# Second mixer of a two-layer encoder: a head's eight 64-by-64 products in two visits to TensorE instead of four

## The chip, the cores and the metric

One Trainium2 chip, one of its cores. The metric is the device time in microseconds (us) of one execution of the whole program. A core has TensorE (PE in the profile; its weight loads have a row of their own, PEld), VectorE (DVE), ScalarE (ACT), GpSimd (POOL) and SyncE (SP), which here issues the loads of weights. Each engine works through its own instructions in the order in which the program holds them, and semaphores tie the engines together.

## The reference

A trunk of two layers over 256 tokens of width 2048, all in float32. A layer is a token mixer and a gated MLP with a short convolution, each behind an RMSNorm and with a residual. The first mixer is a bidirectional mLSTM, the second, which is touched here, a bidirectional HGRN2 with 16 heads of 128 keys and 128 values:

```python
def hgrn_mixer(hn, w_in, lb, head_g, w_out):
    b, s, _ = hn.shape
    p = hn @ w_in
    q, i, g, f_f, f_b = jnp.split(p, [B_F, B_F + B_V, B_F + 2 * B_V, 2 * B_F + 2 * B_V], axis=-1)
    log_lb, log_1mlb = jnp.log(lb), jnp.log1p(-lb)

    def gate(f):
        f = f.astype(jnp.float32)
        log_f = jnp.logaddexp(log_lb, log_1mlb + jax.nn.log_sigmoid(f))
        k = (1.0 - lb) * jax.nn.sigmoid(-f)
        return (k.reshape(b, s, B_HEADS, B_DK), log_f.reshape(b, s, B_HEADS, B_DK))
    ...
    y = hgrn_direction(q, k_f, lf_f, v) + fl(hgrn_direction(fl(q), fl(k_b), fl(lf_b), fl(v)))
    y = y.reshape(b, s, B_V).astype(hn.dtype)
    y = head_rmsnorm(y, head_g, B_HEADS) * jax.nn.silu(g)
    return y @ w_out
```

In each direction a head's output at token t is the sum over the tokens s before it (and t itself) of v[s], weighted by the sum over keys of q[t] k[s] times the product of all forget gates between s and t.

## The kernel before

All the large products (projections, MLPs) take float32 weights from memory in pieces of 128 by 1024. ACT rounds a piece to `wh` (L146), the DVE makes the rest `wl` (L147), and TensorE multiplies both with activations that are split the same way. There are four buffers each for `wh` and `wl` (WB). The projections run in chunks: "fm" chunks (features by tokens, L197 and L198, four contraction tiles in a piece) and "tm" chunks (tokens by features, L187 to L189, two in a piece). In the second mixer each of four groups of four heads has six "fm" chunks (q and two gates a head), one "tm" chunk for the values ahead of the fourth of them, and one "tm" chunk for the output gate at the end. These chunks are the dense matmuls of this text.

Beside the dense stream runs side work, written as generators. A `yield` hands over how much later the generator goes on; the stream's clock (`side.tick`) moves by a fixed amount with each contraction tile. A scheduler that comes with the language then orders the instructions of each engine by its own estimate of times, so the order on an engine isn't quite that of the code.

The side work of a head (function `head` in `hgrn`) computes the 128-by-128 attention blocks AT without ever dividing by a product of gates. It goes up a tree of block sizes h = 1, 2, 4, ... 64 (LEVELS). At each level the DVE multiplies the q and k of half of the blocks by the gates of the neighbouring half (the scalings, L648 and L649, in place in QK), POOL multiplies gates pairwise to those of twice the block size (L654), and the DVE gathers the needed halves to fresh buffers `km` and `qm` (L606). TensorE then forms from them a product of four 64-by-64 matmuls into `pd` (L614). A product of q with ks, the sum of both directions' keys, gives the diagonal; ACT copies it to AD (L632), and the six levels below 64 are merged in by predicated copies under a mask (L640, DVE). The seventh level and AD go to AT on ACT (L643, L644). With the products for q and ks that makes eight products a head, 128 in all.

They are sent in four visits: the diagonal with level 1, then levels 2 and 4, 8 and 16, 32 and 64, and between visits the DVE works on the next two levels. A visit's turn comes `2 * SPREAD` ticks after the one before (`2 * STEP` for the last two heads). The gathers have four buffers each (MIX). After the fourth visit come two 128-by-128 products for the tokens of the other half (L658, L659, the state products), then, once the values are there, the y products (L671), a head norm, the output gate (L686), a transpose `pz` (L692) and the split into `yb` (L204, L205), the input of the output projection. Heads don't wait for each other: head 1 is pushed when its last gate is there, while head 0 is on its way, and so on in pairs.

Of the kernel before, what the change touches and what calls it, by code (L numbers as in the profile page):

```python
# [8 lines left out]
F32 = mybir.dt.float32  # L9
F32R = mybir.dt.float32r  # L10
I32 = mybir.dt.int32
AF = mybir.ActivationFunctionType
ALU = mybir.AluOpType
PSUM = bass.MemoryType.PSUM

P = 128
T = 256
# [6 lines left out]
BH = 16  # L24
# [15 lines left out]
STEP = 1.9  # L40
SPREAD = 2.4
LOOK = 3
RAW = 3
WB = 4
MIX = 4
FIRST = (0, 1, 2, 4, 7, 10, 13, 16)

HALF = 64
LEVELS = (1, 2, 4, 8, 16, 32, HALF)
C_ID, C_MF, C_MB, C_LV = 0, 128, 384, 640  # L50
# [3 lines left out]
def trunk_kernel(ctx, tc, xT, pp_d, cst_d, w_first, w_aq, w_ak, w_av, w_ao, w_aout,  # L54
                 w_bq, w_bv, w_bg, w_bout, w_up, w_down, out, mscr, stop=9):
    nc = tc.nc
    act, dve, pool, pe = nc.scalar, nc.vector, nc.gpsimd, nc.tensor
# [8 lines left out]
    cst = keep.tile([P, NCST], F32, name="cst")  # L66
# [11 lines left out]
    def aux(name):  # L78
        return psa.tile([P, 512], F32, tag="aux", name=name)
# [132 lines left out]
    def fm_scaled(ps, R, dst, scale=None):  # L212
        fm_sum(ps, dst)
        if scale is None:
            dve.tensor_tensor(dst, dst, R, ALU.mult)
        else:
            dve.scalar_tensor_tensor(dst, dst, scale, R, ALU.mult, ALU.mult)
# [75 lines left out]
    def head_scale(ss, width):  # L293
        rs = ev.tile([P, 2], F32, tag="rs", bufs=6, name="rs")
        dve.tensor_scalar(rs, ss, 1.0 / width, EPS, ALU.mult, ALU.add)
        pool.tensor_tensor(rs, rs, hmx, ALU.pow)
        return rs
# [238 lines left out]
    def hgrn(norm, nxt):  # L536
# [24 lines left out]
        def blocks(z, h, a, b):  # L561
            v = z[:, 0:2 * (T + h)].rearrange("k (p x) -> k p x", p=2)[:, :, a:b]
            return v.rearrange("k p (m j) -> k m p j", j=2 * h)[:, :, :, 0:h]

        def gview(g, n, start, h):
            v = g[:, start:start + 2 * (n - 1)].rearrange("k (p x) -> k p x", p=2)[:, :, 0::2]
            return v.rearrange("k p m -> k m p").unsqueeze(3).broadcast_to([P, n // 2, 2, h])

        def take(hd, what, ps):
            mp = box["mp"]  # L570
            st = heads[hd]
            if what == 0:
                st["q"] = mp.tile([P, T], F32, tag="q", bufs=2, name="q")
                fm_scaled(ps, norm.R, st["q"], box["oml"][:, hd:hd + 1])
                st["QK"] = mp.tile([P, 1152], F32, tag="QK", bufs=2, name="QK")
                st["G"] = mp.tile([P, 768], F32, tag="G0", bufs=2, name="G")
                return
            dr = what - 1
            lb, oml = box["lb"], box["oml"]
            QZ, KZ, G = st["QK"][:, 0:512], st["QK"][:, 512:1024], st["G"]  # L580
            z = mp.tile([P, T], F32, tag="z", bufs=2, name="z")
            fm_scaled(ps, norm.R, z)
            g = G[:, dr * T:(dr + 1) * T]
            kz = KZ[:, dr * T:(dr + 1) * T]
            act.activation(g, z, AF.Sigmoid)
            act.activation(kz, z, AF.Sigmoid, scale=-1.0)
            dve.tensor_scalar(g, g, oml[:, hd:hd + 1], lb[:, hd:hd + 1], ALU.mult, ALU.add)
            pool.tensor_tensor(QZ[:, (1 - dr) * T:(2 - dr) * T], st["q"], g, ALU.mult)
            if dr == 0:
                pool.tensor_copy(G[:, 512:768], g)  # L590
            else:
                st["ks"] = mp.tile([P, T], F32, tag="ks", bufs=2, name="ks")
                pool.tensor_tensor(st["ks"], KZ[:, 0:T], KZ[:, T:2 * T], ALU.add)
                side.push(head(hd))

        def head(hd):
            mp = box["mp"]
            st = heads[hd]
            QZ, KZ = st["QK"][:, 0:640], st["QK"][:, 512:1152]
            q, ks, G = st["q"], st["ks"], st["G"]  # L600
            AT = mp.tile([P, 4, P], F32, tag="AT", bufs=2, name="AT")
            AD = mp.tile([P, 2, HALF], F32, tag="AD", bufs=2, name="AD")

            def gather(z, h, tag):
                m = mp.tile([P, T], F32, tag=tag, bufs=MIX, name=tag)
                dve.tensor_copy(m.rearrange("k (m p j) -> k m p j", p=2, j=h), blocks(z, h, 0, T))  # L606
                return m

            def product(pd, k, q, flip=0):

                for b in range(4):
                    o, c = b % 2 * HALF, b // 2 * HALF
                    e = b ^ flip
                    pe.matmul(pd[o:o + HALF, c:c + HALF], k[:, b * HALF:(b + 1) * HALF], q[:, e * HALF:(e + 1) * HALF],  # L614
                              start=True, stop=True)

            def both(ps):
                return ps.rearrange("p (a b) -> p a b", a=2)

            step = 2 * (SPREAD if hd < BH - 2 else STEP)  # L620
            ms = [(gather(KZ, 1, "km"), gather(QZ, 1, "qm"))]
            n = T
            for v in range(4):
                pd = aux("pd")
                if v == 0:
                    product(pd[:, 0:P], ks, q)
                for i, (km, qm) in enumerate(ms):
                    h = LEVELS[max(0, 2 * v - 1) + i]
                    w = i if v else 1
                    product(pd[:, w * P:(w + 1) * P], km, qm, h == HALF)  # L630
                if v == 0:
                    act.copy(AD, both(pd[:, 0:P]))  # L632
                for i in range(len(ms)):
                    li = max(0, 2 * v - 1) + i
                    h = LEVELS[li]
                    w = i if v else 1
                    src = both(pd[:, w * P:(w + 1) * P])
                    if h < HALF:
                        mask = cst[:, C_LV + li * HALF:C_LV + (li + 1) * HALF].bitcast(I32)
                        dve.copy_predicated(AD, mask.unsqueeze(1).broadcast_to([P, 2, HALF]), src)  # L640
                    else:
                        for o in (0, HALF):
                            act.copy(AT[o:o + HALF, 0::3, HALF - o:P - o], src[o:o + HALF])  # L643
                            act.copy(AT[o:o + HALF, 0::3, o:o + HALF], AD[o:o + HALF])  # L644
                ms = []
                for h in LEVELS[2 * v:2 * v + 2] if v < 3 else LEVELS[6:]:
                    qa, ka = blocks(QZ, h, 0, T), blocks(KZ, h, 0, T)
                    dve.tensor_tensor(ka, ka, gview(G, n, 1, h), ALU.mult)  # L648
                    dve.tensor_tensor(qa, qa, gview(G, n, n + 1, h), ALU.mult)  # L649
                    if h < HALF:  # L650
                        ms.append((gather(KZ, 2 * h, "km"), gather(QZ, 2 * h, "qm")))
                        n //= 2
                        G2 = mp.tile([P, 3 * n], F32, tag=f"G{h}", bufs=2, name="G2")
                        pool.tensor_tensor(G2, G[:, 0:6 * n:2], G[:, 1:6 * n:2], ALU.mult)  # L654
                        G = G2
                yield step
            pd = aux("pd")
            pe.matmul(pd[:, 0:P], KZ[:, 0:P], QZ[:, T + P:2 * T], start=True, stop=True)  # L658
            pe.matmul(pd[:, P:T], KZ[:, T + P:2 * T], QZ[:, 0:P], start=True, stop=True)  # L659
            act.copy(AT[:, 1:3], pd[:, 0:T].rearrange("p (a b) -> p a b", a=2))  # L660
            yield
            while "V" not in st["qd"]:
                yield
            V, j = st["qd"]["V"], hd % 4
            py = aux("py")
            y = mp.tile([P, T], F32, tag="y", bufs=4, name="y")
            ss = mp.tile([P, 2], F32, tag="ss", bufs=2, name="ss")
            for t in range(2):
                c = slice(t * P, (t + 1) * P)
                for s in range(2):  # L670
                    pe.matmul(py[:, c], AT[:, 2 * s + t], V[:, s, j * P:(j + 1) * P], start=(s == 0), stop=(s == 1))  # L671
            act.copy(y, py[:, 0:T])
            for t in range(2):
                jk = ev.tile([P, T], F32, tag="jk", bufs=1, name="jk")
                act.activation(jk[:, 0:P], y[:, t * P:(t + 1) * P], AF.Square, accum_out=ss[:, t:t + 1])
            st["y"] = (y, head_scale(ss, 128))
# [19 lines left out]
        heads = [dict() for _ in range(BH)]  # L696
# [197 lines left out]
```

## Time and profile before

| | |
|---|---|
| median of 3 runs | 2480.95 us (2479.69 to 2481.21) |
| the profiled execution | 2482.74 us, span 2480.9 us |
| granted TensorE clock, mean | 0.997 |
| DMA | 448.88 MB, mean 181 GB/s |
| first and last gather `km` (L606) | 1143.3 and 1650.4 us |
| first and last state product (L658) | 1174.6 and 1654.0 us |
| product matmuls (L614), records | 896 for levels, 128 for q and ks |

The profile describes one execution. Its page gives the span, the busy time of each engine, and the chain of work that ended last. A row of the timeline has the start in us, the length in us, the engine, the line of the kernel, the operation, output and inputs by name, and how many records were merged (x8); square brackets show how long the engine sat idle ahead of it and what ended that. A float32 matmul or weight load leaves two records where the operands are plain float32. Matmuls overlap in their pipeline, so the cost of one is read from start to start, and not from its length. In rows by group the columns are count, busy us and mean ns of one, then idle time ahead of the group and what ended it.

### The profile page before, as it was taken

Reading aid. Unit: us, or ns where it says so; the run is one execution under the profiler, and the core shown is the slowest. Engines: PE = TensorE matmul, PEld = TensorE weight load, DVE = VectorE, ACT = ScalarE, POOL = GpSimd, SP = SyncE. Lnnn points to the kernel's source line nnn. Section 1 sums busy time; section 2 is a strip of 40 time slices with the busy share of each in tenths; the row PEclk is TensorE's granted clock in tenths of the full one; section 3 lists DMA queues with packets and bytes.
Section 4 is the critical chain, followed back from the end, with each engine's and each line's share of the span. In section 5 each row is a group of like instructions: output and inputs, shape, how many; then the busy total and the mean of one; then the engine's idle time right before and its main releaser. Section 6 shows DMA issues by size and latency. Waiting matters only on the chain.

```text
span 2480.9 us, 37013 instructions
## 1 busy us (share of the span) xinstructions
PE 2461.8 (99%) x14462; PEld 2114.1 (85%) x14462; DVE 1762.4 (71%) x2943; ACT 1221.2 (49%) x1890; POOL 273.6 (11%) x325
## 2 busy tenths in 40 slices
PE   9999999999999999999999999999999999999998
PEld 7888888888888888887888888888888888888887
DVE  7766677777656777668787878787777765677754
ACT  6555455544444445444454445445544444444443
POOL 0100031000000000122221222224000000000022
PEclk9999999999999999999999999999999999999999
DMA  7655555555555555555444444445555555555553
GB/s 264 191 175 173 175 178 190 192 187 187 191 188 196 189 187 188 186 188 171 153 153 163 160 153 155 154 151 188 186 189 192 194 184 192 189 189 194 187 189 123
DMA packets 65921, 448.88 MB, mean 181 GB/s; under 512 B 7617, under 2 KB 8257, under 8 KB 15569
## 3 DMA queue, kind: packets, MB, share of 16 engines
q1 hardware_dynamic: 63936, 443.03, 53.6%
q0 software_dynamic: 800, 2.16, 0.6%
q8 instruction: 113, 1.85, 0.3%
q10 hardware_dynamic: 1008, 1.32, 0.1%
q14 instruction: 64, 0.52, 0.1%
HBM read 444.32 MB, written 2.16 MB: 180 GB/s over the span
## 4 chain that ended last, share of the span: by engine, by line
PE 96%; DVE 2%; ACT 1%; issue 0%; DMA 0%; SPq 0%; DVEq 0%; POOL 0%; ACTq 0%; POOLq 0%
PE mm L197 52%; PE mm L198 26%; PE mm L189 4%; PE mm L188 4%; PE mm L187 4%; PE pd L614 2%; DVE wl L147 1%; PE pn L440 1%; PE py L671 1%; PE mm L176 1%; DVE QK L648 0%; ACT wh L146 0%; PE S L426 0%; DVE qm L606 0%; DMA raw<-in_w_first 0%
## 5 line engine op out<-in xcount | busy, mean ns | idle before, releaser
L147 DVE TENSOR_TENSOR wl<-raw,wh 128x1024 fp32r<-128x1024 f32 (+1 forms) x864 | 1048.1, 1214 | 577.6 <-ACT wh L146 564.5
L197 PE MATMUL mm<-xt,wh 128*128 128x512 f32 x3776 | 1319.6, 395 | 0.0
L146 ACT CAST wh<-raw 128x1024 fp32r<-128x1024 f32 (+1 forms) x864 | 884.3, 1024 | 854.9 <-PE mm L197 476.6
L198 PE MATMUL mm<-xt,wl 128*128 128x256 f32 x3776 | 1050.7, 278 | 0.0
L197 PEld LDWEIGHTS mm<-xt,wh 128*128 128x128 f32 x3776 | 708.0, 188 | 163.7
L198 PEld LDWEIGHTS mm<-xt,wl 128*128 128x128 f32 x3776 | 710.0, 188 | 1.2
L197 PE MATMUL mm<-g,wh 128*128 128x512 f32 x1334 | 462.6, 394 | 0.0
L198 PE MATMUL mm<-g,wl 128*128 128x256 f32 x1334 | 369.5, 277 | 0.0
L197 PEld LDWEIGHTS mm<-g,wh 128*128 128x128 f32 x1334 | 250.1, 188 | 58.1
L198 PEld LDWEIGHTS mm<-g,wl 128*128 128x128 f32 x1334 | 250.4, 188 | 0.0
L187 PE MATMUL mm<-wh,xt 128*128 128x512 f32 x512 | 204.8, 403 | 2.4 <-ACT xt L204 1.9
L188 PE MATMUL mm<-wl,xt 128*128 128x512 f32 x512 | 203.7, 398 | 0.4 <-DVE wl L147 0.4
L189 PE MATMUL mm<-wh,xt 128*128 128x512 f32 x512 | 202.6, 397 | 0.0
L209 ACT COPY b<-mm 128x256 f32<-128x256 f32 x237 | 87.6, 370 | 178.5 <-PE mm L198 178.5
L243 POOL TENSOR_TENSOR acc<-hx 128x256 f32<-128x256 f32 x4 | 4.7, 1185 | 1242.2 <-DVE hx L312 1242.2
L187 PEld LDWEIGHTS mm<-wh,xt 128*128 128x128 f32 x512 | 96.0, 189 | 22.5 <-ACT xt L204 2.2
L189 PEld LDWEIGHTS mm<-wh,xt 128*128 128x128 f32 x512 | 96.8, 189 | 20.2
L188 PEld LDWEIGHTS mm<-wl,xt 128*128 128x128 f32 x512 | 96.9, 189 | 20.0 <-DVE wl L147 0.8
L197 PE MATMUL mm<-yb,wh 128*128 128x512 f32 x256 | 90.6, 399 | 0.0
L197 PE MATMUL mm<-ya,wh 128*128 128x512 f32 x256 | 89.1, 394 | 0.0
L246 POOL TENSOR_TENSOR sq<-hx 128x256 f32<-128x256 f32 x52 | 63.4, 1226 | 199.1 <-DVE hx L312 196.9
L210 DVE TENSOR_TENSOR a<-mm,b 128x256 f32<-128x256 f32 x86 | 36.5, 425 | 50.6 <-ACT b L209 50.5
(187 smaller groups left out, 2032.1 us busy)
## 6 DMA issues: line engine op xcount, KB each, us to landing
raw<-in_w_up SPq DMA_DIRECT2D x172, 1024.0 KB, 4.9
raw<-in_w_down SPq DMA_DIRECT2D x64, 1024.0 KB, 4.8
raw<-in_w_bq SPq DMA_DIRECT2D x48, 1024.0 KB, 4.9
raw<-in_w_ao SPq DMA_DIRECT2D x16, 1024.0 KB, 4.8
raw<-in_w_aout SPq DMA_DIRECT2D x16, 1024.0 KB, 4.9
raw<-in_w_bv SPq DMA_DIRECT2D x16, 1024.0 KB, 4.8
raw<-in_w_bg SPq DMA_DIRECT2D x16, 1024.0 KB, 4.9
raw<-in_w_bout SPq DMA_DIRECT2D x16, 1024.0 KB, 4.9
```

The costliest lines, as they stand in the source:

```text
L146: act.copy(wh[:, :m], r)
L147: dve.tensor_tensor(wl[:, :m], r, wh[:, :m].bitcast(F32), ALU.subtract)
L176: pe.matmul(ps[f][:, 0:T], w[:, c:c + P], x[:, o:o + T], start=(k + kk == 0 and i == 0), stop=(k + kk == ch.nk - 1 and i == 2))
L187: pe.matmul(ps[t], xh, wh[:, c], start=st, stop=False)
L188: pe.matmul(ps[t], xh, wl[:, c], start=False, stop=False)
L189: pe.matmul(ps[t], xl, wh[:, c], start=False, stop=sp)
L197: pe.matmul(ps[f], wh[:, c:c + P], x, start=st, stop=False)
L198: pe.matmul(ps[f][:, 0:T], wl[:, c:c + P], x[:, 0:T], start=False, stop=sp)
L209: act.copy(b, ps[:, T:2 * T])
L210: dve.tensor_tensor(dst, ps[:, 0:T], b, ALU.add)
L246: eng.tensor_tensor(s, hT[k], hT[k], ALU.mult)
L614: pe.matmul(pd[o:o + HALF, c:c + HALF], k[:, b * HALF:(b + 1) * HALF], q[:, e * HALF:(e + 1) * HALF], start=True, stop=True)
```

## The change

The seven levels are now walked in one loop, one level a step, and a step takes `SPREAD` ticks (`STEP` for the last two heads). The products go out in two visits of four. The first follows the scalings of level 4 and holds the levels 4, 2, 1 and then q with ks; the second follows the last step and holds the levels 64, 32, 16 and 8. In each the level whose gather comes last is sent first. Each visit fills one whole `pd` of 512 columns. The predicated copies run in ascending order of levels as before. MIX goes from 4 to 5. A head doesn't begin before the head ahead of it has sent its second visit (`done`). The state products, y products and all else stay as they were; lines from L658 of the kernel before on stand one line earlier after.

```diff
-MIX = 4
+MIX = 5
...
             st = heads[hd]
+            while hd and "done" not in heads[hd - 1]:
+                yield 0.3
...
-            step = 2 * (SPREAD if hd < BH - 2 else STEP)
-            ms = [(gather(KZ, 1, "km"), gather(QZ, 1, "qm"))]
-            n = T
-            for v in range(4):
-                pd = aux("pd")
-                if v == 0:
+            step = SPREAD if hd < BH - 2 else STEP
...
+            ms, n = [(gather(KZ, 1, "km"), gather(QZ, 1, "qm"))], T
+            yield step
+            for li, h in enumerate(LEVELS):
+                qa, ka = blocks(QZ, h, 0, T), blocks(KZ, h, 0, T)
+                dve.tensor_tensor(ka, ka, gview(G, n, 1, h), ALU.mult)
+                dve.tensor_tensor(qa, qa, gview(G, n, n + 1, h), ALU.mult)
+                if h < HALF:
+                    ms.append((gather(KZ, 2 * h, "km"), gather(QZ, 2 * h, "qm")))
+                    n //= 2
+                    G2 = mp.tile([P, 3 * n], F32, tag=f"G{h}", bufs=2, name="G2")
+                    pool.tensor_tensor(G2, G[:, 0:6 * n:2], G[:, 1:6 * n:2], ALU.mult)
+                    G = G2
+                if li == 2:
+                    pd = aux("pd")
+                    for i in (2, 1, 0):
+                        product(pd[:, (i + 1) * P:(i + 2) * P], *ms[i])
                     product(pd[:, 0:P], ks, q)
-                for i, (km, qm) in enumerate(ms):
-                    h = LEVELS[max(0, 2 * v - 1) + i]
-                    w = i if v else 1
-                    product(pd[:, w * P:(w + 1) * P], km, qm, h == HALF)
-                if v == 0:
                     act.copy(AD, both(pd[:, 0:P]))
...
+                    for i in range(3):
+                        dve.copy_predicated(AD, mask[i], both(pd[:, (i + 1) * P:(i + 2) * P]))
                 yield step
+            pd = aux("pd")
+            for i in (6, 5, 4, 3):
+                product(pd[:, (i - 3) * P:(i - 2) * P], *ms[i], i == 6)
+            for i in (3, 4, 5):
+                dve.copy_predicated(AD, mask[i], both(pd[:, (i - 3) * P:(i - 2) * P]))
+            src = both(pd[:, 3 * P:4 * P])
+            st["done"] = True
+            for o in (0, HALF):
+                act.copy(AT[o:o + HALF, 0::3, HALF - o:P - o], src[o:o + HALF])
+                act.copy(AT[o:o + HALF, 0::3, o:o + HALF], AD[o:o + HALF])
```

More of the change, by code (lines that the diff above doesn't have):

```diff
@@ L618, in both @@
                 return ps.rearrange("p (a b) -> p a b", a=2)
-            step = 2 * (SPREAD if hd < BH - 2 else STEP)
-            ms = [(gather(KZ, 1, "km"), gather(QZ, 1, "qm"))]
-            n = T
-            for v in range(4):
-                pd = aux("pd")
-                if v == 0:
-                    product(pd[:, 0:P], ks, q)
-                for i, (km, qm) in enumerate(ms):
-                    h = LEVELS[max(0, 2 * v - 1) + i]
-                    w = i if v else 1
-                    product(pd[:, w * P:(w + 1) * P], km, qm, h == HALF)
-                if v == 0:
-                    act.copy(AD, both(pd[:, 0:P]))
[L633 to L655, printed above, removed]
-                yield step
@@ new lines, in head @@
+            step = SPREAD if hd < BH - 2 else STEP
+            mask = [cst[:, C_LV + i * HALF:C_LV + (i + 1) * HALF].bitcast(I32).unsqueeze(1).broadcast_to([P, 2, HALF])
+                    for i in range(6)]
+            ms, n = [(gather(KZ, 1, "km"), gather(QZ, 1, "qm"))], T
[14 more added lines that the diff above has]
+                        product(pd[:, (i + 1) * P:(i + 2) * P], *ms[i])
+                    product(pd[:, 0:P], ks, q)
+                    act.copy(AD, both(pd[:, 0:P]))
+                    for i in range(3):
+                        dve.copy_predicated(AD, mask[i], both(pd[:, (i + 1) * P:(i + 2) * P]))
+                yield step
```

## The prediction

> **What bounds the kernel now.** I read the page first: the span, the busy times and the chain that ended last.
>
> ```profile
> span 2480.9 us, 37013 instructions
> PE 2461.8 (99%) x14462; PEld 2114.1 (85%) x14462; DVE 1762.4 (71%) x2943; ACT 1221.2 (49%) x1890; POOL 273.6 (11%) x325
> PE 96%; DVE 2%; ACT 1%; issue 0%; DMA 0%; SPq 0%; DVEq 0%; POOL 0%; ACTq 0%; POOLq 0%
> ```
>
> TensorE is never free and the chain runs along it, so the question is what each microsecond of it is spent on. The change touches only the second mixer, so next came busy times by stretch (columns: length, PE, PEld, DVE, ACT, POOL, granted clock, DMA share, GB/s).
>
> ```profile
> 1136.00:1660.00 524.00, 520.09 (x3443) 423.17 (x3442) 428.48 (x884) 254.00 (x465) 132.36 (x175) 1.00 0.47 155
> 1146.00:1164.00 18.00, 17.98 (x119) 13.82 (x118) 17.97 (x40) 7.30 (x12) 9.97 (x12) 1.00 0.36 118
> ```
>
> In the mixer's 524 us the DVE is at 82%, well above the 71% of the whole, and in the first 18 us of head work it is full. TensorE ends the chain, the DVE stands close behind.
>
> The timeline of TensorE tells what a visit of 64-by-64 products costs. A product is four instructions and eight records, since each float32 matmul is recorded twice. First the dense cadence, then one product alone:
>
> ```profile
> 1229.66 0.39 PE L188 MATMUL mm<-wl,xt 128*128 128x512 f32 x1
> ...
> 1234.42 0.39 PE L188 MATMUL mm<-wl,xt 128*128 128x512 f32 x1
> ```
> ```profile
> 1155.21 0.39 PE L189 MATMUL mm<-wh,xt 128*128 128x512 f32 x1
> 1155.53 0.45 PE L614 MATMUL pd<-qm,km 128*64 128x64 f32 x8
> 1155.91 0.50 PE L187 MATMUL mm<-wh,xt 128*128 128x512 f32 x1
> 1156.24 0.39 PE L188 MATMUL mm<-wl,xt 128*128 128x512 f32 x1
> ```
>
> Between 1229.66 and 1234.42 lie 21 intervals: 0.227 us a dense matmul. From 1155.21 to 1156.24 are 1.03 us where two intervals would be 0.45, so a lone product costs **0.576 us**: the way in (0.32 instead of 0.23), the products, and a way out that slows even the following matmul (0.33).
>
> Now products in a row (the timeline cut at 1235.25), then a whole group of four, and two rows of its weight loads:
>
> ```profile
> 1235.02 0.40 PE L614 MATMUL pd<-qm,km 128*64 128x64 f32 x8
> ```
> ```profile
> 1302.11 0.39 PE L188 MATMUL mm<-wl,xt 128*128 128x512 f32 x1
> 1302.43 0.45 PE L614 MATMUL pd<-q,ks 128*64 128x64 f32 x8
> 1302.71 0.51 PE L614 MATMUL pd<-qm,km 128*64 128x64 f32 x10
> 1303.64 0.69 PE L614 MATMUL pd<-qm,km 128*64 128x64 f32 x14 [0.42 <-DVE qm L606]
> 1304.26 0.50 PE L189 MATMUL mm<-wh,xt 128*128 128x512 f32 x1
> 1304.59 0.39 PE L187 MATMUL mm<-wh,xt 128*128 128x512 f32 x1
> ```
> ```profile
> 1301.88 0.19 PEld L188 LDWEIGHTS mm<-wl,xt 128*128 128x128 f32 x1
> 1302.42 0.31 PEld L614 LDWEIGHTS pd<-q,ks 128*64 128x64 f32 x8 [0.35 <-issue]
> ```
>
> Eight records, one product, start inside 1235.02 to 1235.25: a further product in the same visit adds 0.24 us. So 0.576 − 0.24 = **0.336 us is the price of entering and leaving**, paid once a visit. A group of four should cost 0.576 + 3 × 0.24 = 1.30 us. The one at 1302 took 2.48 − 0.45 = 2.03: it waited 0.73 us, in its middle, for a gather.
>
> **The change, part by part.** The orders of the two built programs hold the same instructions on each engine; DMAs and SP's queue are the same too. Only places differ, and only between the second mixer's start and the first columns of its output projection. So no operation is added or removed, and the sum is made of entries, waits and places.
>
> *Entries.* In the order before, TensorE's 128 products stand in 103 visits: 76 lone ones, 8 groups of four, the rest singly beside the state products (L658, L659) or the y products (L671). In the order after they stand in 33: 31 whole groups of four, and one cut 1 + 3 by two transposes. 70 entries fewer, 70 × 0.336 = **−23.5 us**. Bounds: 0 if the price comes back (a rival below), −25 if the way out costs a little more. The state products ride on a visit after as most did before, and the y products still come about four in a visit: nothing for both.
>
> *Waits that go.* The first group of four is the costly one:
>
> ```profile
> 1164.38 0.39 PE L188 MATMUL mm<-wl,xt 128*128 128x512 f32 x1
> 1164.70 0.45 PE L614 MATMUL pd<-q,ks 128*64 128x64 f32 x8
> 1164.98 0.40 PE L614 MATMUL pd<-qm,km 128*64 128x64 f32 x8
> 1166.25 0.34 PE L614 MATMUL pd<-qm,km 128*64 128x64 f32 x4 [0.86 <-DVE qm L606]
> 1167.44 0.91 PE L614 MATMUL pd<-qm,km 128*64 128x64 f32 x12 [0.86 <-DVE qm L606]
> 1168.28 0.80 PE L189 MATMUL mm<-wh,xt 128*128 128x512 f32 x1
> ...
> 1170.92 0.40 PE L189 MATMUL mm<-wh,xt 128*128 128x512 f32 x1
> ```
> ```profile
> 1168.30:1170.80 2.50, 2.50 (x8) 2.02 (x7) 2.50 (x9) 1.61 (x4) 0.00 (x0) 0.50 0.64 269
> ```
>
> From 1164.38 to 1170.92 are 6.54 us; seven dense intervals and one group of four make 1.59 + 1.30 = 2.89. So 3.65 us went here, partly in two waits of 0.86 and partly because the granted clock then stood at 0.50. Of the other seven groups five look like the one at 1302 (0.73 each) and two waited 0.34 (at 1234 and 1504). In all 3.65 + 5 × 0.73 + 2 × 0.34 = **8.0 us of waits**.
>
> How many stay? The orders say where a visit stands against the weight pieces (one `wl` of L147 each, about 2.8 us of TensorE). Before, 53 products need a gather that stands behind the `wl` of two pieces further on than the piece TensorE is at, 52 of one piece; after, none needs more than one piece further. That is a whole piece more of cover. Against it stands the DVE's load. These rows are of the mixer alone, 1146 to 1662:
>
> ```profile
> L147 DVE TENSOR_TENSOR wl<-raw,wh 128x1024 fp32r<-128x1024 f32 x152 | 191.5, 1260 | 66.7 <-ACT wh L146 66.0
> L648 DVE TENSOR_TENSOR QK<-QK,G 128x256 f32<-128x256 f32 x111 | 57.4, 518 | 0.0
> L649 DVE TENSOR_TENSOR QK<-QK,G 128x256 f32<-128x256 f32 x112 | 53.4, 477 | 0.1
> L606 DVE COPY qm<-QK 128x256 f32<-128x256 f32 x112 | 39.0, 348 | 0.5 <-POOL QK L588 0.5
> L640 DVE COPY_PREDICATED AD<-cst,pd 128x128 f32<-128x128 int32 x96 | 27.4, 292 | 3.1 <-PE pd L614 2.9
> ```
>
> The densest eight pieces of the order before hold 8 `wl`, 23 gathers, 25 scalings, 11 predicated copies and 6 operations on new gates (about 0.42 each): 10.1 + 8.0 + 12.4 + 3.2 + 2.5 = 36 us. The densest after hold 19 gathers, 19 scalings, 9 copies and about 4.4 us of others: 33 us. TensorE needs about 22 us for the dense part of eight pieces, plus the visits. The heads one behind another flatten the load, though it stays over TensorE's.
>
> *A wait that is added.* Seven gathers a head in five buffers (MIX) must wait for the visit that frees a buffer. Before, 14 gathers stand on the DVE waiting for TensorE, after 35. Queued behind each are scalings, gathers and the next `wl`, for which TensorE's dense matmuls wait; but that `wl` is always that of four or five pieces further on, about as far as the four `wl` buffers let the DVE run, so nothing is late at once. What it costs is the DVE's chance to work ahead. Bounds for what remains of waiting: 0, and 33 × 0.73 = 24 us if every visit waits like the group at 1302. I take **4 us**, half of today's, since cover grew and load fell, but the DVE is held more often.
>
> *Transposes.* Ten more of them stand alone between dense matmuls:
>
> ```profile
> 1662.75 0.39 PE L197 MATMUL mm<-yb,wh 128*128 128x512 f32 x1
> ...
> 1663.09 0.40 PE L197 MATMUL mm<-yb,wh 128*128 128x512 f32 x1
> 1663.33 0.27 PE L692 MATMUL pz<-cst,y 128*128 128x128 f32 x1
> 1663.36 0.36 PE L198 MATMUL mm<-yb,wl 128*128 128x256 f32 x1
> 1663.56 0.40 PE L197 MATMUL mm<-yb,wh 128*128 128x512 f32 x1
> ```
>
> A pair takes 0.34, with a transpose 0.47: 10 × 0.13 = **+1.3 us**.
>
> *The last head* comes later: its second visit now falls into the output projection. There the order after lets the second column's matmuls run while the last `yb` is missing, and 17 dense pairs (17 × 0.34 = 5.8 us) stand between the last y products and their transposes, so I give it 0; uncovered, a few us.
>
> Sum: −23.5 − 8.0 + 4 + 1.3 = −26.2 us. The profiled execution took 2482.74 (span 2480.9 and 1.8 around it), so 2456.5; the median of the runs shown is 1.8 lower, so I forecast **2455**.
>
> **The rivals.**
>
> 1. *Every visit waits.* With 33 large visits each behind its last gather, TensorE could stand 0.73 us at each: −23.5 − 8.0 + 24 + 1.3 = −6 us, **2475**. For it: the groups of four before are just where the waits were, while lone products hardly waited. Against: the deeper cover.
>
> 2. *The entries cost nothing.* If the weight loads of a lone product ran under the matmuls ahead of it, or if each product in a large visit paid its own way in, no entry would be saved: −8.0 + 4 + 1.3 = −3 us, **2478**. The Trainium skill, "TensorE: Matmul & The Clock Gate", section "Step-by-step: what each phase is for", speaks for it: TensorE pulls weight loads ahead of running matmuls. The trace here doesn't agree: the load at 1302.42 starts 0.31 us after the last dense matmul did. And 0.24 us for the second product in a row is measured. Little remains for it.
>
> 3. *Slower: heads one behind another don't fit.* First and last start of the gathers and of the state products (ns of one: least, median, most; then the starts in us):
>
> ```profile
> L606 DVE COPY km<-QK x112: 274/282/891, 1143.3 to 1650.4; 128x256 f32<-128x256 f32 x112
> L658 PE MATMUL pd<-QK x32: 270/275/377, 1174.6 to 1654.0; 128*128 128x128 f32 x32
> ```
>
> Head 0 took 1174.6 − 1143.3 = 31.3 us from its first gather to its state product, and heads follow each other every (1654.0 − 1174.6) / 15 = 32.0 us. Before, two heads share the time; after, a head starts when the one ahead has sent its last products. If a head alone took 34 us, 16 heads would be 16 × 2 = 32 us late, TensorE would stand for most of it, and −26 + 32 = +6 gives **2487**. It decides from 32 us a head upwards. Against it: head 0 ran while the DVE was full with head 1 as well. A head's own DVE work is 14 × 0.35 + 7 × (0.518 + 0.477) + 6 × 0.292 = 13.6 us, with eight `wl` 10.1 more: 24 us.
>
> That the change doesn't do what it says is excluded by the order for the grouping.
>
> **How the numbers follow.** About 0.2% (5 us) is what a measurement of this kernel can tell from no change. The forecast has 0.70 (its own range 2447 to 2463), rival 1 0.14, rival 2 0.07, rival 3 0.09. The range that should hold 8 in 10 reaches from no waits left and a dearer entry (−25 − 8 + 1.3 = −32, 2449, less a little) to rival 1 and holds it: 2447 to 2476. Faster by over 0.2%: the forecast and nearly all of rival 1, 0.84; within 0.2%: rival 2, 0.07; slower: 0.09.
>
> **What would show it.** In the changed profile a visit should be 32 records in a row, with 1.30 + 0.45 = 1.75 us from the dense matmul ahead of it to the second one behind and at most a little wait, all of it at its head; the waits of L616 for gathers should sum to some 4 us, and the first heads should show no stretch at half clock. If the second product in a visit starts much later than 0.24 us after the first, the entries came back. If the dense matmuls wait for `wl` in the mixer, the added DVE waits decided. If the mixer (first gather to last state product, 511 us before) isn't some 25 us shorter, the prediction is wrong.

## The result, and the profile after

The changed kernel takes **2451.92 us** (median of 4 runs, 2451.01 to 2452.68), the kernel before, on the same chip, 2481.08 (2479.69 to 2481.97). The ratio is 0.9883, with a 95% interval of 0.9866 to 0.9900: 29.2 us faster. The profiled execution took 2451.01 us, so from profile to profile the gain is 31.7.

From the page after: the span, the busy times, and the chain by engine.

```profile
span 2449.2 us, 36986 instructions
PE 2432.1 (99%) x14462; PEld 2108.3 (86%) x14462; DVE 1759.7 (72%) x2943; ACT 1221.2 (50%) x1890; POOL 267.4 (11%) x325
PE 98%; DVE 1%; ACT 0%; issue 0%; DMA 0%; SPq 0%; POOL 0%; DVEq 0%; POOLq 0%
```

The span is 31.7 us shorter, with the same 14462 matmul records. TensorE's share of the chain went from 96% to 98%, the DVE's from 2% to 1%. The busy times of the other engines moved by some 6 us at most.

Where the time left shows at the first and last matmul on the output projection's input (the group of `mm<-yb,wh`, before and then after; after the count come least, median and most ns of one, then first and last start).

```profile
L197 PE MATMUL mm<-yb,wh x256: 387/398/481, 1658.0 to 1749.7; 128*128 128x512 f32 x128
```
```profile
L197 PE MATMUL mm<-yb,wh x256: 387/395/500, 1625.7 to 1718.3; 128*128 128x512 f32 x128
```

The first starts 32.3 us earlier, the last 31.4. All of it is gained in the second mixer. By stretch, from the first gather to the output projection (before, then after; columns as in the prediction, with the granted clock third from the end):

```profile
1143.30:1658.00 514.70, 510.79 (x3386) 414.89 (x3385) 421.56 (x872) 246.45 (x453) 132.34 (x175) 1.00 0.47 156
```
```profile
1143.60:1626.50 482.90, 481.68 (x3355) 409.06 (x3354) 416.73 (x867) 245.73 (x450) 127.46 (x175) 1.00 0.49 165
1146.00:1164.00 18.00, 18.00 (x114) 14.99 (x113) 17.96 (x37) 8.37 (x14) 9.95 (x13) 1.00 0.35 119
1164.00:1172.00 8.00, 6.78 (x60) 5.46 (x59) 8.00 (x16) 2.02 (x4) 3.15 (x6) 1.00 0.50 144
```

Nearly the same matmuls and the same DVE work stand in 482.9 instead of 514.7 us. TensorE's own idle time in it was only 3.9 us and is now 1.2; the rest of the gain was never idle time in the profile, but busy time that did no work. The two short rows are of the first heads: the DVE is still full there, but the clock stays at 1.00 in the stretch that had some 3.4 us at half clock before (1167.44 to 1170.80).

A visit after (timeline of TensorE):

```profile
1217.00 0.39 PE L188 MATMUL mm<-wl,xt 128*128 128x512 f32 x1
1217.32 0.92 PE L616 MATMUL pd<-qm,km 128*64 128x64 f32 x24
1218.07 0.40 PE L616 MATMUL pd<-q,ks 128*64 128x64 f32 x8
1218.40 0.50 PE L189 MATMUL mm<-wh,xt 128*128 128x512 f32 x1
1218.74 0.39 PE L187 MATMUL mm<-wh,xt 128*128 128x512 f32 x1
```

The 32 records are in a row, and from the dense matmul ahead to the second one behind are 1218.74 − 1217.00 = 1.74 us, where 1.75 were forecast. The way in (0.32) and the slowed matmul behind (0.34) are there once. The only visit with a wait that the profile marks:

```profile
1165.24 0.39 PE L189 MATMUL mm<-wh,xt 128*128 128x512 f32 x1
1166.43 1.15 PE L616 MATMUL pd<-qm,km 128*64 128x64 f32 x32 [0.80 <-DVE qm L608]
1168.00 0.46 PE L657 MATMUL pd<-QK 128*128 128x128 f32 x2 [0.41 <-DVE QK L630]
...
1168.75 0.40 PE L188 MATMUL mm<-wl,xt 128*128 128x512 f32 x1
```

It is the second visit of head 0, and the wait is at its head, for the gather that is sent first. The view of waits has these two rows for TensorE in the whole mixer (total us, times, longest; first that of before for gathers, then after):

```profile
PE pd L614 <- DVE qm L606: 3.8, 7, 0.9
```
```profile
PE pd L616 <- DVE qm L608: 0.8, 1, 0.8
PE pd L657 <- DVE QK L630: 0.4, 1, 0.4
```

### The profile page after: what moved, and what is told of

Its sections match the earlier page's. It is cut to its first block, busy times and chain, and to the rows that moved or that the text cites. A ratio compares the mean times of both kernels' runs of the same rounds, so it can differ in the third digit from the quotient of the medians.

```text
span 2449.2 us, 36986 instructions
## 1 busy us (share of the span) xinstructions
PE 2432.1 (99%) x14462; PEld 2108.3 (86%) x14462; DVE 1759.7 (72%) x2943; ACT 1221.2 (50%) x1890; POOL 267.4 (11%) x325
## 4 chain that ended last, share of the span: by engine, by line
PE 98%; DVE 1%; ACT 0%; issue 0%; DMA 0%; SPq 0%; POOL 0%; DVEq 0%; POOLq 0%
PE mm L197 53%; PE mm L198 26%; PE mm L187 5%; PE mm L189 5%; PE mm L188 5%; PE pd L616 1%; PE pn L440 1%; PE mm L176 1%; PE py L670 1%; DVE wl L147 0%; PE S L426 0%; PE pd L657 0%; DMA raw<-in_w_first 0%; DVE QK L629 0%; PE pz L691 0%
## 5 line engine op out<-in xcount | busy, mean ns | idle before, releaser
L197 PE MATMUL mm<-xt,wh 128*128 128x512 f32 x3776 | 1319.5, 395 | 0.0
L198 PE MATMUL mm<-xt,wl 128*128 128x256 f32 x3776 | 1049.9, 278 | 0.0
L197 PEld LDWEIGHTS mm<-xt,wh 128*128 128x128 f32 x3776 | 708.3, 188 | 164.3
L198 PEld LDWEIGHTS mm<-xt,wl 128*128 128x128 f32 x3776 | 710.1, 188 | 0.8
L197 PE MATMUL mm<-g,wh 128*128 128x512 f32 x1334 | 462.6, 394 | 0.0
L198 PE MATMUL mm<-g,wl 128*128 128x256 f32 x1334 | 369.5, 277 | 0.0
L197 PEld LDWEIGHTS mm<-g,wh 128*128 128x128 f32 x1334 | 250.1, 188 | 58.0
L198 PEld LDWEIGHTS mm<-g,wl 128*128 128x128 f32 x1334 | 250.5, 188 | 0.0
L187 PE MATMUL mm<-wh,xt 128*128 128x512 f32 x512 | 201.9, 398 | 3.1 <-ACT xt L204 2.5
L189 PE MATMUL mm<-wh,xt 128*128 128x512 f32 x512 | 200.6, 393 | 0.0
L189 PEld LDWEIGHTS mm<-wh,xt 128*128 128x128 f32 x512 | 96.5, 188 | 19.9
L197 PE MATMUL mm<-yb,wh 128*128 128x512 f32 x256 | 89.6, 396 | 0.0
L197 PE MATMUL mm<-ya,wh 128*128 128x512 f32 x256 | 89.1, 394 | 0.0
```

Of the source, the lines that this page charges most:

```text
L187: pe.matmul(ps[t], xh, wh[:, c], start=st, stop=False)
L189: pe.matmul(ps[t], xl, wh[:, c], start=False, stop=sp)
L197: pe.matmul(ps[f], wh[:, c:c + P], x, start=st, stop=False)
L198: pe.matmul(ps[f][:, 0:T], wl[:, c:c + P], x[:, 0:T], start=False, stop=sp)
```

## The experiments

The theory: the gain is 70 entries to product visits at 0.34 us or a little more, and the waits, which the heads' order removes. The rivals: the entries cost nothing and the order does it all; or the grouping costs waits that the buffers hide. The experiments ran on other chips than the result; the kernel before took 2481.6 to 2482.1 us there and 2481.1 here, so a difference to the 2451.92 of the changed kernel is good to about 1 us.

**Heads one behind another alone.** The kernel before, with one thing of the change: a head waits for the one ahead. Its products stand in 99 visits.

```diff
 # the kernel before
+            while hd and "done" not in heads[hd - 1]:
+                yield 0.3
...
+            st["done"] = True
```

> The kernel before with one thing of the change alone: a head does not begin until the head ahead has sent its last products. Four visits a head stay; in the order of TensorE the products stand in 99 visits (103 before, 33 after the change). Theory of the entries (each visit costs 0.336 us beside its products, and the rest of the gain is waits): 4 entries fewer are -1.3 us, and at most the 8 us of waits can go, so 2472 to 2480 us. Rival (heads one behind another flatten the DVE's load and this alone is the gain): about 2455 us.

Measured: 2475.97 us (2475.39 to 2478.49, 10 runs) against 2482.06 of the kernel before, ratio 0.9978 (0.9968 to 0.9987). The products are L616 in this kernel. In the mixer the view of waits has no row in which TensorE's matmuls wait for a gather. The weight loads of the products do have gaps, none over 0.4 us, about as long as the 0.35 ahead of the first load of the visit at 1302.42 before. About half are put down to no wait that the profile shows ("issue"), the rest to work of the DVE, nine of them to gathers:

```profile
PEld pd L616 <- issue: 12.4, 43, 0.4
PEld pd L616 <- DVE km L608: 1.3, 5, 0.4
PEld pd L616 <- DVE qm L608: 1.1, 4, 0.4
```

So the order of the heads is worth 6 us. That is less than the 8.0 us of waits and the 4 entries that go with it, and the difference wasn't assigned. The other 24 us of the change come with the grouping, to which the fifth buffer and the order of sending belong.

**Each product by itself.** The changed kernel, but every level sends its product as soon as it can: 139 visits, no waits for gathers.

```diff
 # the changed kernel
-                if li == 2:
+                if li == 0:
                     pd = aux("pd")
-                    for i in (2, 1, 0):
-                        product(pd[:, (i + 1) * P:(i + 2) * P], *ms[i])
                     product(pd[:, 0:P], ks, q)
...
+                yield step / 2
+                pd = aux("pd")
+                product(pd[:, 0:P], *ms[li], h == HALF)
...
+                yield step / 2
```

> The changed kernel with each of the eight products of a head sent by itself, a level behind its gather; heads stay one behind another, MIX stays 5. In the order the products stand in 139 visits. Theory of the entries: 106 more than after the change, 106 x 0.336 = +35.6 us on 2451.9, so 2487 us, up to 2492 with waits; slower than the kernel before. Rival (the gain is from heads one behind another and from the earlier gathers): within 5 us of the changed kernel, 2447 to 2457 us.

Measured: 2491.56 us (2491.34 to 2491.68), ratio 1.0038 (1.0023 to 1.0053). It has the order of heads and is still slower than the kernel before. That rules out that the order alone did it, or that entries are free. 36 entries more than before at 0.34 to 0.36 make some 13 us, less the 8 us of waits; of the 9.5 us measured, 4 to 5 weren't assigned.

**The entry by itself.** 80 needless products of a constant tile go into the two MLPs, far from any gather, once as 80 lone products and once as 20 groups of four. The work added is equal; the entries differ by 60.

```diff
 # the changed kernel, in the "fm" chunks
                         side.tick(0.325 * len(ps))
+                        if k == 8 and ch.extra:
+                            px = aux("px")
+                            for j in range(ch.extra):      # 1, or 4 in every fourth chunk
+                                for b in range(4):
+                                    o, c = b % 2 * HALF, j * P + b // 2 * HALF
+                                    pe.matmul(px[o:o + HALF, c:c + HALF], ones[:, 0:HALF], ones[:, HALF:P],
+                                              start=True, stop=True)
```

> The changed kernel with 80 needless 64-by-64 products of a constant tile added in the MLPs, where no gather is near, each alone between dense matmuls (40 a layer; the result is not read). Theory of the entries: 80 x 0.576 = +46 us, 2498 us. Rival (what a lone product costs is mostly waiting for its gather, or its loads hide under dense matmuls): 80 x 0.24 = +19 us or less, 2471 us.

> The same 80 needless products in 20 groups of four (10 a layer). Theory of the entries: 20 x 1.30 = +26 us, 2478 us, so 20 us less than with lone ones (60 entries x 0.336). Rival (a product costs the same wherever it stands): the same time as with lone ones.

Measured: 2523.58 us lone (2523.28 to 2526.78, ratio 1.0170, 1.0155 to 1.0185) and 2503.65 in fours (2503.07 to 2505.21, ratio 1.0088, 1.0073 to 1.0103). The difference is 19.9 us: 60 entries at **0.332 us**, as expected. One of each, from the two timelines:

```profile
525.43 0.28 PE L198 MATMUL mm<-xt,wl 128*128 128x256 f32 x1
525.63 0.45 PE L205 MATMUL px<-ones 128*64 128x64 f32 x8
526.02 0.50 PE L197 MATMUL mm<-xt,wh 128*128 128x512 f32 x1
526.35 0.28 PE L198 MATMUL mm<-xt,wl 128*128 128x256 f32 x1
```
```profile
499.58 0.28 PE L198 MATMUL mm<-xt,wl 128*128 128x256 f32 x1
499.79 1.15 PE L205 MATMUL px<-ones 128*64 128x64 f32 x32
500.87 0.50 PE L197 MATMUL mm<-xt,wh 128*128 128x512 f32 x1
501.20 0.28 PE L198 MATMUL mm<-xt,wl 128*128 128x256 f32 x1
```

Where a dense pair takes 0.35, there are 0.92 with one product and 1.62 with four. But both kernels are 26 us above what was expected of them. That isn't the probes: 80 × 0.576 and 20 × 1.28 us are what their rows show. It is the dense pairs between them, and the last section is about that.

**More visits.** Three a head (52 visits): the second visit of the changed kernel is cut in two.

```diff
 # the changed kernel
+                if li == 4:
+                    pd = aux("pd")
+                    for i in (4, 3):
+                        product(pd[:, (i - 3) * P:(i - 2) * P], *ms[i])
...
-            for i in (6, 5, 4, 3):
+            for i in (6, 5):
```

> The changed kernel with the second visit cut in two (levels 16 and 8, then 64 and 32): 52 visits in the order. Theory of the entries: 19 more x 0.336 = +6.4 us, 2458 us. Rival (only the waits count, and smaller visits wait less): 2452 us or less.

Measured: 2459.79 us (2458.03 to 2461.69), ratio 0.9911 (0.9896 to 0.9926), where 2481.62 is the kernel before. That is 7.9 us over the changed kernel, where 19 entries were to cost 6.4. Smaller visits aren't quicker.

**The level that is ready first, sent first.** Only the order within a visit is turned round; the scheduler then draws products away from their groups, and there are 44 visits.

```diff
 # the changed kernel
-                    for i in (2, 1, 0):
+                    for i in (0, 1, 2):
...
-            for i in (6, 5, 4, 3):
+            for i in (3, 4, 5, 6):
```

> The changed kernel with the products of a visit sent in the order in which their gathers come (levels 1, 2, 4 and 8, 16, 32, 64) instead of the last one first. The scheduler then cuts many first visits in two: 44 visits instead of 33. Theory of the entries: 11 x 0.336 = +3.7 us plus some waits inside visits, 2455 to 2459 us. Rival (the order of sending is what took the waits away): waits of 0.73 us at each visit come back, +24 us, 2475 us.

Measured: 2457.6 us (2457.11 to 2458.13), ratio 0.9903 (0.9886 to 0.9920). Waits in this trace:

```profile
PE pd L657 <- POOL G L635: 1.2, 1, 1.2
PE pd L616 <- DVE qm L608: 0.8, 3, 0.4
```

Together they are 2.0 us, 0.8 more than in the changed kernel; 11 entries make 4. That is most of the 5.7 us. So the order of sending isn't what took the waits away; sending the late level first pays above all by keeping a group together in the scheduler's order; what the order is worth with the visits as they are wasn't tried.

**One visit a head, and its buffers alone.** All eight products go in one visit (17 visits), the first four into a second tile. That needs seven gather buffers (MIX), and to make room the pairwise gates and z have one buffer each. The second kernel has those buffers and the two visits of the change.

```diff
 # both
-MIX = 5
+MIX = 7
-            z = mp.tile([P, T], F32, tag="z", bufs=2, name="z")
+            z = mp.tile([P, T], F32, tag="z", bufs=1, name="z")
-                    G2 = mp.tile([P, 3 * n], F32, tag=f"G{h}", bufs=2, name="G2")
+                    G2 = mp.tile([P, 3 * n], F32, tag=f"G{h}", bufs=1, name="G2")
 # one visit
-                if li == 2:
...
-            pd = aux("pd")
+            p0, pd = aux("p0"), aux("pd")
             for i in (6, 5, 4, 3):
                 product(pd[:, (i - 3) * P:(i - 2) * P], *ms[i], i == 6)
+            for i in (2, 1, 0):
+                product(p0[:, (i + 1) * P:(i + 2) * P], *ms[i])
+            product(p0[:, 0:P], ks, q)
```

> The changed kernel with all eight products of a head in one visit at its end (MIX 7; to make room the pairwise gates and z have one buffer instead of two). 17 visits instead of 33. Theory of the entries: 16 x 0.336 = -5.4 us, 2446.5 us, if no waits come. Rival (the visit then holds the DVE's gathers of the next head and the merging of seven levels comes in one lump, so TensorE waits): 2452 us or more.

> The changed kernel with two visits and the buffers of the one-visit kernel (MIX 7, one buffer for the pairwise gates and for z): 32 visits. It says what the buffers alone do. Theory of the entries: same as after the change, 2450 to 2454 us. If the wait that was added (gathers that wait for the visit that frees a buffer) cost something, seven buffers take it away and it is faster by up to 2 us.

Measured: one visit 2443.6 us (2442.71 to 2444.64), ratio 0.9846 (0.9831 to 0.9861), better than both kernels; the buffers alone 2450.97 (2450.55 to 2451.65), ratio 0.9876 (0.9861 to 0.9891). So two more buffers for the gathers, with one less for gates and z, change nothing that is clear of noise. That fits the view of waits: in the mixer of the changed kernel no instruction of the DVE has a marked wait for TensorE. The wait for a free gather buffer, which the change adds to the program, doesn't show. A visit of one head:

```profile
1252.28 1.15 PE L616 MATMUL pd<-qm,km 128*64 128x64 f32 x32
1253.26 0.87 PE L616 MATMUL p<-qm,km 128*64 128x64 f32 x24
1253.96 0.40 PE L616 MATMUL p<-q,ks 128*64 128x64 f32 x8
1254.29 0.49 PE L655 MATMUL pd<-QK 128*128 128x128 f32 x2
1254.62 0.39 PE L656 MATMUL pd<-QK 128*128 128x128 f32 x2
```

64 records in a row, nothing waiting, with the state products on the same visit. In the whole mixer of this kernel TensorE has two marked waits, of 0.3 and 0.4 us, so the rival (TensorE waits) is out.

The gain over the changed kernel is 8.3 us and 5.4 were expected. 16 entries fewer at 0.36 (worked out below) make 5.8. The rest fits with the dense pairs of this mixer, which ran a little quicker: from start to start 348.6 ns in the mean against 351.8 in the changed kernel (worked out from the starts, pairs that have dense matmuls on both sides), on 768 pairs 2.5 us.

Over the kernels with heads in a row, from 17 visits at 2443.6 us to 139 at 2491.6, a visit costs 48.0 / 122 = 0.39 us; from the changed kernel's 33 to the 99 of the first experiment 24.1 / 66 = 0.365, and the kernels with 44 and 52 visits lie within 2 us of that line. Time follows the number of visits, through everything else that differs.

**Four that missed: moving visits into the pairs.** The probes had shown that dense pairs behind a probe run slower. My theory was that it depends on the place, behind the second matmul of a pair (L198) and not behind the first (L197). Four kernels tested it: the probes between the two matmuls of a pair, from the first chunk on or only after two chunks, and the changed kernel and the one-visit kernel with the turn of the side work moved to that place.

```diff
 # lone probes: the same lines, inside the pair
-                        if k == 8 and ch.extra:
+                            if f and k == 8 and ch.extra:
...
-                chunks[-1].extra = 1 * (f0 + i < 40 and (f0 + i) % 1 == 0)
+                chunks[-1].extra = 1 * (f0 + i < 40)            # first kernel
+                chunks[-1].extra = 1 * (2 <= f0 + i < 42)       # second kernel
```
```diff
 # the changed kernel, and the one-visit kernel
+                            if f:
+                                side.tick(0.325 * len(ps))
...
-                        side.tick(0.325 * len(ps))
```

> The kernel with 80 lone needless products again, each now between the two matmuls of a dense pair (behind L197, ahead of L198) instead of between two pairs (behind L198). With the products between pairs the time was 2523.6 us, 26 us more than 80 x 0.576; in its trace the dense pairs of the MLPs take 353 us per thousand instead of 347 from the first such product on. Theory of the beat (a visit behind L198 leaves the pairs behind it at 353 ns, one behind L197 at 347): 2451.9 + 46 = 2498 us and pairs at 347 ns. Rival (80 products cost 72 us wherever they stand, by another cause such as the extra PSUM tiles): about 2523 us.

> The 80 lone needless products behind L197 again, with the first two chunks of each MLP left free, so that the first product does not come right behind the norm's small matmuls that stand behind an L198. In the run before it (2524.9 us) the pairs went to 353 ns at that first product already, and each later product found them there. Theory (a visit behind L197 leaves the beat as it finds it, one behind L198 sets the slow one): the MLPs stay at 347 ns a pair, 2451.9 + 80 x 0.576 = 2498 us. Rival (any product sets the slow beat, wherever it stands): 2524 us. If the pairs are slow in one MLP and not in the other: about 2511 us, and what sets the beat is still open.

> The changed kernel with the turn of the side work moved inside a dense pair, so that 33 of the visits and y products that stood behind an L198 or an L197 now stand 33 behind L197 and 9 behind L198 (before this edit 18 and 24). Theory of the beat: in the second mixer some 700 pairs have a mean of 351.6 ns, and with most at 347 about 3 us go, 2449 us. Rival (the place inside a pair does nothing): 2452 us.

> One visit a head (2443.6 us) with the turn of the side work inside a dense pair: all 14 visits in such chunks then stand behind L197 (6 before this edit), while 16 y products stay behind L198. Theory of the beat: 1 to 2 us less, 2442 us. Rival: 2443.6 us or more.

Measured: probes inside 2524.91 us (2524.21 to 2525.21, ratio 1.0173, 1.0160 to 1.0187) and 2523.99 (2522.95 to 2524.14, ratio 1.0169, 1.0151 to 1.0187); the changed kernel with the moved turn 2466.5 (2465.32 to 2466.96, ratio 0.9937, 0.9925 to 0.9950), the one-visit kernel with it 2459.07 (2457.84 to 2459.92, ratio 0.9910, 0.9895 to 0.9925). All four missed: the theory of the place is wrong. In the kernel with free first chunks a probe behind L197 switches the pairs, too, and it is the second probe that does so:

```profile
429.10 0.45 PE L203 MATMUL px<-ones 128*64 128x64 f32 x8
...
429.70 0.40 PE L197 MATMUL mm<-xt,wh 128*128 128x512 f32 x1
...
439.77 0.39 PE L197 MATMUL mm<-xt,wh 128*128 128x512 f32 x1
...
440.46 0.39 PE L197 MATMUL mm<-xt,wh 128*128 128x512 f32 x1
440.78 0.45 PE L203 MATMUL px<-ones 128*64 128x64 f32 x8
...
442.09 0.40 PE L197 MATMUL mm<-xt,wh 128*128 128x512 f32 x1
...
443.15 0.40 PE L197 MATMUL mm<-xt,wh 128*128 128x512 f32 x1
```

Behind the first probe 31 pairs take 440.46 − 429.70 = 10.76 us, or 0.347 each, and the last two of them 440.46 − 439.77 = 0.69. Three behind the second probe take 443.15 − 442.09 = 1.06, or 0.353 each. The two probes stand at the same place in a pair, and only one of them switched the pace. In the two kernels with the moved turn, the second mixer by itself, from the last matmul of the first MLP to the first on `yb`, is 0.7 us shorter and 0.3 us longer than without; 3 and 1 to 2 us less were expected. What makes these kernels longer lies ahead of it (last section).

## Why the prediction was right

It gave 2455 us, and 2451.92 was measured, inside its range and inside the narrower one of the forecast; the sign is that of the likeliest case. From profile to profile the sum was −26.2 us and −31.7 was measured. The entries were 1.6 us too small and the waits 2.8, both to the same side, so it didn't come out right by errors that cancel. The 4 us of waits that were to stay were a choice between bounds, and a poor one. Step by step:

- *TensorE bounds the mixer, and its busy time holds the loss.* Right: the gain of 31.7 us holds only 2.7 us of idle time that the profile marks.
- *70 entries at 0.336.* Right in kind, a little small. The probes measured 0.332 by their times. In the mixer the 76 lone visits of before cost 45.1 us more than dense work (0.593 each, with the slowed matmul behind), and the 15 whole visits of four that stand by themselves after cost 1.298 each. With e for the entry and p for a product, e + p = 0.593 and e + 4p = 1.298 give p = 0.235 and e = 0.358, so the term is −25.1 and not −23.5. These are means, and a few slow visits raise them: 8 of the lone ones take 0.67, 3 of the groups 1.37. The medians, 0.581 and 1.281, give p = 0.233 and e = 0.348, close to the 0.342 that the median rows of the two probe kernels give (0.575 and 1.275). What holds up the few wasn't followed.
- *8.0 us of waits go, 4 stay.* The first part is borne out by the heads in a row alone, which removed every marked wait of a matmul on a gather and brought 6 us. The second was mis-sized: 1.2 us of marked waits stay, all at head 0. The prediction had the heads in a row flatten the DVE's load. The rows don't show that: from 1146 to 1172 the DVE is as full as before, and over the mixer its share rose, from 421.56 of 514.70 us (82%) to 416.73 of 482.90 (86%). From head 1 on no visit has a marked wait all the same. The cover of a whole piece more fits that, but it wasn't tried by itself.
- *The added wait of gathers for buffers costs nothing that shows.* Right: no marked wait of the DVE for TensorE in the mixer, and no change clear of noise by the buffers alone.
- *Transposes +1.3.* Right: stretches with transposes alone went from 2.2 us in 11 to 3.4 in 21.
- *The last head 0.* Right: in the view of waits TensorE's mixer has nothing beyond head 0.

With the measured sizes the sum is −25.1 − 6.8 + 1.2 = −30.7 us, where the trace has −31.7. The 1 us that is left wasn't assigned.

The rivals. That every visit waits: one did. That the entries cost nothing: excluded by the kernel with each product by itself and by the 60 entries of the probes; a product between dense matmuls takes 0.576 us here and one in a row 0.235. The Trainium skill, "TensorE: Matmul & The Clock Gate", section "Step-by-step: what each phase is for", has TensorE pull weight loads ahead of running matmuls, on conditions (row groups that don't conflict, or a load into the background weight buffer). The prediction said that the trace doesn't agree, which is too broad: in its own rows the dense load at 1301.88 comes 0.23 us ahead of its matmul at 1302.11, as the skill has it, and only the first load of the visit, at 1302.42, comes with its matmul at 1302.43. Why that one isn't early no run here shows. That heads one behind another don't fit: head 0 now takes 1168.00 − 1143.60 = 24.4 us from its first gather to its state product, close to the 24 us that the prediction counted as a head's DVE work, and under the (1634.1 − 1168.0) / 15 = 31.1 us at which heads follow each other. The changed kernel without the heads' wait wasn't tried, so what the grouping does without that order isn't shown.

One mark that the prediction set was a bad one: from first gather to last state product the mixer is only some 20 us shorter (490.5, the last state product after starts at 1634.1), where it asked for some 25. The last head was moved into the output projection, so its state product now has dense work ahead of it that stood behind it before. The first matmul on `yb` is the better mark.

## What to carry to other kernels

On an engine that is always busy, look for busy time that does no work: read the cost of a small piece from start to start, from the dense matmul ahead to the second one behind, once alone and once in a row; the difference is what every switch costs, and here the grouping brought some 24 of 29 us. Holding small products back for a group can bring waits for the last operand, so look for them: here, with a head at a time, one of 33 visits had a marked one. Measure such a price away from the place where it is claimed (equal work, other grouping), and look at the dense work beside the probe as well.

## What wasn't expected of the hardware

**Two paces of the same dense pairs.** The pairs of L197 and L198 in the MLPs run at one of two paces, at a granted clock of 1.00 and with no wait. By stretch in the first MLP, where no product visit is near, the changed kernel and then the same with the moved turn:

```profile
600.00:1000.00 400.00, 400.00 (x2309) 349.81 (x2309) 267.44 (x406) 188.61 (x265) 0.00 (x0) 1.00 0.57 189
```
```profile
600.00:1000.00 400.00, 400.00 (x2266) 346.94 (x2265) 261.07 (x395) 185.32 (x259) 0.00 (x0) 1.00 0.55 186
```

2309 matmuls against 2266 in 400 us: 346.5 and 353.1 ns a pair. Once there, the slow pace holds to the end of the MLP. With lone probes it came with the first of them (timeline of that kernel):

```profile
414.15 0.40 PE L197 MATMUL mm<-xt,wh 128*128 128x512 f32 x1
...
415.19 0.39 PE L197 MATMUL mm<-xt,wh 128*128 128x512 f32 x1
415.43 0.28 PE L198 MATMUL mm<-xt,wl 128*128 128x256 f32 x1
415.54 0.61 PE L293 MATMUL pr<-dg,ones 128*128 128x128 f32 x4
416.07 0.45 PE L205 MATMUL px<-ones 128*64 128x64 f32 x8
...
417.27 0.40 PE L197 MATMUL mm<-xt,wh 128*128 128x512 f32 x1
...
418.33 0.40 PE L197 MATMUL mm<-xt,wh 128*128 128x512 f32 x1
```

Three pairs ahead take 1.04 us, three behind 1.06. On the some 3900 (lone) and 4000 (in fours) pairs of both MLPs that stand between dense matmuls 6.6 ns each make 26 us, which is the whole miss of both probe kernels. In the two kernels with the moved turn the pairs are slow from 323 us, in the first mixer's output projection, to the end of the first MLP, although no visit of the second mixer falls into that. These some 2300 pairs make 15 us, and the two kernels are 14.6 and 15.5 us longer than those without the moved turn. In the kernels before and after, both MLPs are at the quick pace. What sets the pace, and what sets it back, stays open. It isn't the place within a pair alone, as the two probes at 429.10 and 440.78 showed.

**Half clock after short idle times.** Before, the clock was halved after two waits of 0.86 us within 3 us, in which TensorE was busy for 1.02 of 2.74 us:

```profile
1164.70:1167.44 2.74, 1.02 (x21) 0.74 (x21) 2.74 (x6) 0.00 (x0) 2.50 (x4) 0.99 0.37 54
1167.44:1168.30 0.86, 0.86 (x13) 0.74 (x13) 0.86 (x2) 0.12 (x1) 0.34 (x2) 0.50 0.71 267
```

In the 3.40 us from 1164.00 to 1167.40, up to the halving, TensorE was busy for 1.72. After, one wait of 0.80 us and one of 0.41 left it at 1.00, with 2.18 us busy in the 3.40 from 1164.60 to 1168.00. What decides between the two no run here shows. The Trainium skill, "TensorE: Matmul & The Clock Gate", section "What's actually happening", has the halving after an idle window of about 3.4 us; this trace shows it after less idle time than that.
